# Fixing TensorE's issue order across the turns of an interleaved mixer stage, and moving a row load and a branch hint in the expert stage

## Chip, core, metric

One core of a Trainium2 chip runs the whole program as a single launch. The metric is device time in microseconds (us). TensorE (PE in the rows; PEld is its weight load) does the matmuls, VectorE (DVE) and ScalarE (ACT) the element-wise work, GpSimd (POOL) some element-wise work and some transfers, SyncE (SP) issues most transfers. Each engine takes its own queue in order.

## What is computed

Three blocks follow one another on a sequence of 512 tokens with 1024 features, in float32:

```
for l in range(2):
    p = h @ w_in[l]                                   # 3888 columns
    ya, yb = hgrn2(pa), gla(pb)                       # chunked gated linear attention
    yc = rwkv7(pc)                                    # delta-rule recurrence
    yd = retention(pd)                                # chunked, with rotary
    h = layer_norm(ALPHA * h + concat(ya, yb, yc, yd) @ w_out[l])
    f = swiglu(h) if l == 0 else moe(h)               # 8 experts, top 2 of them
    h = layer_norm(ALPHA * h + f)
h = h + 0.5 * rms_norm(swiglu(rms_norm(h)))           # then a hybrid block:
h = h + rms_norm(concat(rg_lru, window_attention) @ w_o)
h = h + 0.5 * rms_norm(swiglu(rms_norm(h)))
```

Every head of the four mixers of a layer ends in a norm over its 64 features (`rms_norm` or `group_norm`); the keys of rwkv7 are normalized per head as well.

## The kernel before

Activations lie feature-major, as 8 tiles of 128 features by 512 tokens. Weights come as units of 128x1024 over SP's queue (L662, L721 for the experts). Each unit is split into a rounded part on ScalarE and the remainder on VectorE (L353, L354), and a product is three matmuls, high by high, low by high and high by low (L384 to L386; L444 to L447 for the first blocks, L870 to L872 for projections with tokens on the partitions).

**The mixers** (`mixer1`, run for l = 0 and l = 1) are three Python generators that trace instructions: one runs the two rwkv pairs, one the input projections, one the linear attentions (`hg(0)`, `hg(1)`) and retention (`ret`). Each `yield` ends a turn and hands back a cost; `weave` gives the next turn to the stream whose weighted sum of costs is lowest. One turn of the projections is one block of three matmuls. Turns of the other two streams are groups of small products: 32x32 and 64x64 pieces of the chunk solves (L1152, L1092, L1105, L1233), levels of the gated attention (L1343, L1372 to L1411), attention times values (L1423, L1502).

The order in which the weave traces is not the order in which the engines run. A planner places each engine's instructions: it keeps the dependencies and, among what its model takes to be ready, prefers what was traced first. `tc.issue_after(ins)` adds to each instruction that its block traces on the engine of `ins` an edge that puts it behind `ins` in that engine's queue; nobody waits for `ins` to finish by it.

The norm per head is one function, called in one go between two yields (so within one turn), twice in each of the two rwkv pairs (L1058 to L1060 and L1249 to L1250), four times in `hg`, twice in `ret`: 10 calls in each of the two mixers.

```
def head_rstd(self, sq, eps, floor=None):
    s = k.bankB()[:, :P]
    for i in range(NT):
        nc.tensor.matmul(s[32 * i:32 * i + 32], self.bones[:, 48:80], sq[...], ...)      # L924
    nc.scalar.activation(rows, s, AF.Copy)                                               # L926
    nc.tensor.transpose(st, rows, k.ident)                                               # L928
    nc.vector.tensor_scalar(r, st, 1.0 / 64, eps, ...)                                   # L932 (L934 with a floor)
    nc.vector.reciprocal(r, r)                                                           # L935
    nc.scalar.activation(rb, r..., AF.Sqrt)                                              # L936
    for i in range(NT):
        nc.tensor.transpose(R[...], rb[...], k.ident)                                    # L939
```

The output projection of a mixer (`gemm_fm` with `yH`, `yL`) is traced behind the weave and is in no turn.

**The experts** (`experts`): 8 experts one after the other, each with 11 blocks of hidden features (`hidden` for gate and up, L1920 to L1926) and then 11 blocks of the down product (`moe_down`). A block's GpSimd product `rest` (L1935) reads the tiles `mg`, of which there are four; ScalarE's next eviction into `mg` (L1925) needs a free one. Between the blocks `tick` issues side work on GpSimd, in expert 0 the scatter of token rows and gates to DRAM (L1792). `inputs(e + 1)` loads the next expert's rows (L1825, L1827), for expert 1 over GpSimd's own queue, and transposes them on TensorE during the down product (L1836; blocks 4, 6 and 8 in expert 0). In the last block of the last expert every engine loads the largest count of tokens into a register (L1956) and branches around `moe_overflow` (L1957), which runs only where an expert got more than 160 tokens. `combine` follows (L2002 to L2038).

Of the kernel before, what the change touches and what calls it, by code (L numbers as in the profile page):

```python
# [2 lines left out]

# [1 line left out]

# [13 lines left out]
T = 512  # L19
# [7 lines left out]
NE = 8  # L27
# [4 lines left out]
LIM = CAP  # L32
# [700 lines left out]
WEAVEA = (1.0, 1.4, 1.8)  # L733
WEAVEB = (1.0, 1.3, 1.8)
NH32 = 4
WARM = 10
AHEAD = 1
STEP, LAG, LEAD = 4, 12, 4
RINGD, RINGO = 10, 8
LAG1, LEAD1, LAG2 = 12, 2, 18  # L740
LATE = ((0, 2, 4, 6), (0,))
INPUTS, INPUTS0, PLACES = (2, 5, 8), (4, 6, 8), 9
REST, PACE = 4, 8
WARMR = (9, 6)
WARMC = 10
# [45 lines left out]
        return self.pool.tile(shape, dt, name=name, tag=self.tag, bufs=self.bufs)  # L791


def weave(streams, weights):


    at = [0.0] * len(streams)
    live = set(range(len(streams)))
    now = 0.0
    while live:  # L800
        for n in sorted(live, key=lambda i: at[i]):
            try:
                c = next(streams[n])
            except StopIteration:
                live.remove(n)
                break
            if c is not None:
                now = at[n]
                at[n] += c / weights[n]
                break  # L810
            at[n] = max(at[n], now)
# [707 lines left out]
def mixer1(k, l, begin):  # L1519
    tc = k.tc  # L1520
    with tc.tile_pool(name="mxc", bufs=1, reuse_waits="tile") as cp, \
            tc.tile_pool(name="mxa", bufs=1, reuse_waits="tile") as ap, \
            tc.tile_pool(name="mxb", bufs=1, reuse_waits="tile") as bp:
        sl = Slots(ap, "a", NA)
        st = k.stream(f"win{l}")
        if begin:
            k.load_x(sl, st)
        m = Mix(k, l, st, cp, ap, bp)
        if begin:
            trig(k, sl)  # L1530

        def chain(*gens):
            for g in gens:
                yield from g

        weave([chain(m.rwkv_pair(0), m.rwkv_pair(1)),
               chain(m.rwkv_in((6, 2, 0, 4, 5)), m.hg_in(0), m.rwkv_in((7, 8, 3, 1)), m.hg_gate(0), m.hg_in(1),
                     m.hg_gate(1), m.ret_in()),
               chain(m.hg(0), m.hg(1), m.ret())], (WEAVEA, WEAVEB)[l])
        sT = []  # L1540
        for f in range(0, KT, 2):
            t = m.a2(("ZR", "MB")[f // 4], [P, 2, T])
            sT += [t[:, 0], t[:, 1]]
        st = k.ln_stats(sl, 1 if l else 2)
        ws = k.stream(f"wout{l}", *(() if l else (Slots(bp, "b", NB), 0, KT - 2)))
        tot = Totals(*st)
        ys = (lambda q: m.yH[q]), (lambda q: m.yL[q])
        ro = k.moe if l else None
        if ro:
            flat = lambda t: t.rearrange("p a b c -> p (a b c)")  # L1550
            ro.open(sl, *[Cut(flat(m.a2("ZL", [P, NT, 2, P]))) for _ in range(2)])
        for f in range(KT):
            k.resid_in(f, sT)
            if f >= st[0].last and not l:
                continue
            ps = k.gemm_fm(ws, ys, KT, tot.first if f == KT - 1 else None)
            k.resid_out(f, ps, sT, st)
            if ro:
                ro.logits(f, sT[f])
        if ro:  # L1560
            ro.route(sT, tot, ap, m.yH[0])
        else:
            k.ln_end(ws, ys, KT, 2 * KT, sT, k.par(f"ln1g{l}"), k.par(f"ln1b{l}"), sl, st)
        if "y" in k.dbgs:
            for f in range(KT):
                t = sl.tile([P, T])
                k.nc.vector.tensor_tensor(t, m.yH[f].bitcast(F32), m.yL[f].bitcast(F32), op=OP.add)
                k.nc.sync.dma_start(k.dbgs["y"][f], t)
# [26 lines left out]
class Moe:  # L1595
# [251 lines left out]
    def experts(self):  # L1847
# [49 lines left out]
        with tc.tile_pool(name="me", bufs=1, reuse_waits="tile") as me, \  # L1897
                tc.tile_pool(name="mr", bufs=1, reuse_waits="tile") as mr:
            ws = self.ws
            ws.enter(mr)  # L1900
            nxt = self.xe0
            slow = [gains(), residual()]
            for e in range(NE):
                xe = nxt
                beside = [self.scatter(), self.slot_gates(me)] if e == 0 else [clear()] if e == 1 else [collect()] if e == NE - 1 else slow

                def tick(after):
                    with tc.issue_after(after.ins):
                        while beside and next(beside[0], beside) is beside:
                            beside.pop(0)  # L1910

                xf = xe.rearrange("p k w c -> p k (w c)")

                def hidden():
                    ps = k.bankA()[:, :2 * C]
                    for q in range(KT):
                        wH, wL = ws.block()
                        last = q == KT - 1
                        if last:
                            mm(ps[:, :C], wL, xe[:, q, 0], start=False, stop=False, skip_group_check=True)  # L1920
                        mm(ps, wH, xf[:, q], start=q == 0, stop=last, skip_group_check=True)  # L1921
                        if not last:
                            mm(ps[:, :C], wL, xe[:, q, 0], start=False, stop=False, skip_group_check=True)  # L1923
                    a = me.tile([P, C], F32, name="mg", tag="mg", bufs=4)
                    nc.scalar.activation(a, ps[:, C:], AF.Copy)  # L1925
                    V.tensor_tensor(a, ps[:, :C], a, op=OP.add)  # L1926
                    return a

                hid = me.tile([P, NHE, 2, P], F32R, name="hid")
                rest = me.tile([P, NHE, CR], F32, name="rest")  # L1930
                for hb in range(NHE):
                    g = hidden()
                    nc.scalar.activation(g, g, AF.Silu)
                    u = hidden()
                    last = pin(nc.gpsimd.tensor_tensor(rest[:, hb], u[:, P:], g[:, P:], op=OP.mult))  # L1935
                    V.tensor_tensor(u[:, :P], u[:, :P], g[:, :P], op=OP.mult)
                    k.split(u[:, :P], hid[:, hb, 0], hid[:, hb, 1])
                    tick(last)
                    if 0 < e < NE - 1 and hb == NHE - 2:
                        step = self.inputs(e + 1, me)  # L1940
                        next(step)
                if e == 0:
                    step = self.inputs(1, me)
                    next(step)
                if e + 1 < NE:
                    nxt = next(step)

                def side(hb):
                    tick(after[0])
                    if e + 1 < NE and hb in (INPUTS if e else INPUTS0):  # L1950
                        after[0] = next(step)
                    if e + 1 == NE and hb == PLACES:
                        at.append(places())
                    if e + 1 == NE and hb == NHE - 1:
                        with tc.issue_after(ws.last.ins):
                            rv = nc.values_load(self.most[0:1, 0:1], min_val=0, max_val=T)  # L1956
                        with tc.If(rv > LIM):  # L1957
                            moe_overflow(k, h, acc, self.govf, lnrow + [me.tile([P, D], F32, name="yr")])

                at, after = [], [last]  # L1960
                yb, rb = moe_down(k, ws, hid, rest, side)
                gs = [self.gs[:, n, e:e + 1] for n in range(2)]
                if e + 1 < NE:
                    moe_store(k, yb, rb, gs, me, k.yg[e * C:(e + 1) * C])
                else:
                    cp = at[0]
            for n in range(2):
                for w, b in ((0, yb[n]), (1, rb)):
                    if n and w:
                        continue  # L1970
                    hi, lo = cp[:, w, n, 0], cp[:, w, n, 1]
                    nc.scalar.activation(hi, b, AF.Copy, scale=gs[w])
                    V.scalar_tensor_tensor(lo, b, gs[w], hi.bitcast(F32), op0=OP.mult, op1=OP.subtract)
# [83 lines left out]
def moe_down(k, ws, hid, rest, side):  # L2057
# [12 lines left out]
    for hb in range(NHE):  # L2070
# [6 lines left out]
                    r0 = 32 * (2 * n + b % 2)  # L2077
                    mm(rb[r0:r0 + CR], rest[:, b], raws[b][:, n * 512:(n + 1) * 512], start=b < 2, stop=b >= NHE - 2, **kw)
        last = hb == NHE - 1
        side(hb)  # L2080
        (wH, wL), = cut[hb]
        for n in range(2):
            c = slice(n * 512, (n + 1) * 512)
            mm(yb[n], hid[:, hb, 0], wH[:, c], start=hb == 0, stop=False, **kw)
            mm(yb[n], hid[:, hb, 1], wH[:, c], start=False, stop=False, **kw)  # L2085
            mm(yb[n], hid[:, hb, 0], wL[:, c], start=False, stop=last, **kw)
    return yb, rb
# [70 lines left out]
class Second:  # L2158
# [96 lines left out]
    def mixer(self):  # L2255
        k, tc = self.k, self.k.tc
        with tc.tile_pool(name="m2y", bufs=1) as big:
            with tc.tile_pool(name="m2", bufs=1, reuse_waits="tile") as pool:
                m = Hybrid(k, self, big, pool)
                weave([m.project(), m.lru(), m.heads(0), m.heads(1), m.attend()], WEAVE2)  # L2260
            with tc.tile_pool(name="m2o", bufs=1) as p:
                ws = k.stream("wo2", p, RINGO, KT - 2)
                self.post(ws, ((lambda a: m.yH[a]), (lambda a: m.yL[a])), KT, 2, 2 * KT, "mpost", 1.0, "pre2", p, LEAD)
# [289 lines left out]
```

## Time and profile before

| | us |
|---|---|
| runs | 2668.97, 2675.64, 2676.03; median 2675.64 |
| the profiled execution | 2673.79, its span 2672.0 |
| mixers without their first blocks, 28 to 345 and 772 to 1095 | 317 and 323 |
| experts, 1150 to 1720 | 570 |
| TensorE busy | 2599.1 (97%) |
| VectorE, ScalarE, GpSimd busy | 1630.6, 1343.1, 306.6 |

The row of a view gives an engine, the line in the kernel, the operation and the tiles it writes and reads. A wait is put down to the instruction whose end released it; "issue" is time in which an engine waited for nothing that the profile shows, and a q behind an engine's name is its sequencer. PEclk is the mean granted TensorE clock of a stretch: 1.00 is 2.4 GHz, 0.50 is 1.2 GHz.

### The profile page before, as it was taken

To read this page: it belongs to the slowest core of one execution; us is meant where nothing else is said; L and a number is where in the kernel's file an instruction comes from. 1 tells how busy PE (TensorE), PEld (TensorE's weight loads), DVE (VectorE), ACT (ScalarE), POOL (GpSimd) and SP (SyncE) were. 2 spreads that over 40 slices of the span, in tenths; PEclk is the share of its full clock that TensorE was granted. 3 is DMA by queue.
4 is the path that set the end of the run, shared out by engine and by line. 5 is a ranking of instruction groups with operands and counts; after the bars stand their busy time and mean duration, and the time that the engine had idled before them with its cause. 6 is when DMAs were issued, how large, how long until landed. Compare 5 with 4: busy or idle time off the path is not lost. (4 is left out here: it accounts for less than half of the span.)

```text
span 2672.0 us, 48382 instructions
## 1 busy us (share of the span) xinstructions
PE 2599.1 (97%) x18694; PEld 2124.3 (80%) x18694; DVE 1630.6 (61%) x3390; ACT 1343.1 (50%) x2789; POOL 306.6 (11%) x390
## 2 busy tenths in 40 slices
PE   8999999999999999989999999999999999999998
PEld 6776688888877676788888888688888877888887
DVE  6665574444476555557888888665553578655533
ACT  5465354343353554356666776554433467544432
POOL 1101120000031010033233233100000100100000
PEclk9999999999999999999999999899999999999999
DMA  4111422322321112279887888623223212223222
GB/s 160 50 49 50 158 77 97 102 96 95 110 74 43 55 54 69 80 247 288 277 273 268 282 274 266 190 72 102 95 95 100 84 64 77 74 95 101 97 95 71
DMA packets 96330, 334.40 MB, mean 125 GB/s; under 512 B 12079, under 2 KB 15631, under 8 KB 96096
## 3 DMA queue, kind: packets, MB, share of 16 engines
q1 hardware_dynamic: 87520, 305.61, 34.1%
q0 software_dynamic: 8000, 24.95, 3.0%
q8 instruction: 150, 2.46, 0.4%
q10 hardware_dynamic: 576, 0.69, 0.1%
q14 instruction: 84, 0.69, 0.1%
HBM read 313.76 MB, written 17.45 MB: 124 GB/s over the span
## 5 line engine op out<-in xcount | busy, mean ns | idle before, releaser
L353 ACT ACTIVATE whi<-wraw 128x256 fp32r<-128x256 f32 x1172 | 475.6, 415 | 776.7 <-PE bkA L385 706.1
L354 DVE TENSOR_TENSOR wlo<-wraw,whi 128x256 fp32r<-128x256 f32 x1172 | 486.7, 423 | 582.4 <-ACT whi L353 560.1
L384 PE MATMUL bkA<-xH,whi 128*128 128x512 f32 x1352 | 537.4, 397 | 2.1 <-DVE sh L963 1.8
L385 PE MATMUL bkA<-xL,whi 128*128 128x512 f32 x1352 | 535.9, 396 | 0.0
L386 PE MATMUL bkA<-xH,wlo 128*128 128x512 f32 x1352 | 531.9, 393 | 0.0
L1921 PE MATMUL bkA<-xe,mhi 128*128 128x320 f32 x1392 | 361.4, 345 | 10.4 <-ACT mhi L353 8.9
L384 PEld LDWEIGHTS bkA<-xH,whi 128*128 128x128 f32 x1352 | 254.4, 188 | 69.0 <-issue 13.6
L385 PEld LDWEIGHTS bkA<-xL,whi 128*128 128x128 f32 x1352 | 254.8, 188 | 58.4 <-issue 9.6
L386 PEld LDWEIGHTS bkA<-xH,wlo 128*128 128x128 f32 x1352 | 254.4, 188 | 58.4 <-issue 7.0
L1923 PE MATMUL bkA<-xe,mlo 128*128 128x160 f32 x1218 | 289.0, 237 | 2.1 <-DVE mlo L354 2.1
L1921 PEld LDWEIGHTS bkA<-xe,mhi 128*128 128x128 f32 x1392 | 252.0, 190 | 12.2 <-ACT mhi L353 9.5
L1923 PEld LDWEIGHTS bkA<-xe,mlo 128*128 128x128 f32 x1218 | 234.4, 192 | 3.4 <-DVE mlo L354 3.2
L384 PE MATMUL bkA<-hH,whi 128*128 128x512 f32 (+1 forms) x548 | 204.2, 373 | 0.0
L385 PE MATMUL bkA<-hL,whi 128*128 128x512 f32 (+1 forms) x548 | 203.9, 372 | 0.0
L386 PE MATMUL bkA<-hH,wlo 128*128 128x512 f32 (+1 forms) x548 | 203.7, 372 | 0.0
L354 DVE TENSOR_TENSOR mlo<-mraw,mhi 128x1024 fp32r<-128x1024 f32 x105 | 139.9, 1334 | 33.4 <-ACT mhi L353 31.2
L353 ACT ACTIVATE mhi<-mraw 128x1024 fp32r<-128x1024 f32 x105 | 110.3, 1053 | 19.1 <-PE bkA L2085 9.8
L354 DVE TENSOR_TENSOR mlo<-wraw,mhi 128x1024 fp32r<-128x1024 f32 x79 | 104.3, 1323 | 23.7 <-ACT mhi L353 21.8
L385 PEld LDWEIGHTS bkA<-hL,whi 128*128 128x128 f32 x548 | 103.2, 188 | 18.0
L384 PEld LDWEIGHTS bkA<-hH,whi 128*128 128x128 f32 x548 | 103.2, 188 | 18.0
L386 PEld LDWEIGHTS bkA<-hH,wlo 128*128 128x128 f32 x548 | 103.1, 188 | 17.9
L354 DVE TENSOR_TENSOR mlo<-mlow,mhi 128x1024 fp32r<-128x1024 f32 x78 | 105.8, 1358 | 18.3 <-ACT mhi L353 17.0
(738 smaller groups left out, 4428.5 us busy)
## 6 DMA issues: line engine op xcount, KB each, us to landing
mraw<-moew SPq DMA_DIRECT2D x105, 512.0 KB
wraw<-moew SPq DMA_DIRECT2D x81, 512.0 KB
mlow<-moew SPq DMA_DIRECT2D x78, 512.0 KB
wraw<-win SPq DMA_DIRECT2D x76, 512.0 KB
wraw<-f0gu SPq DMA_DIRECT2D x44, 512.0 KB
wraw<-f1gu SPq DMA_DIRECT2D x44, 512.0 KB
wraw<-f2gu SPq DMA_DIRECT2D x44, 512.0 KB
wraw<-f0d SPq DMA_DIRECT2D x22, 512.0 KB
```

The costliest lines, as they stand in the source:

```text
L353: nc.scalar.activation(hi, x, AF.Copy)
L354: nc.vector.tensor_tensor(lo, x, hi.bitcast(F32), op=OP.subtract)
L384: mm(ps, wH, xH, start=first, stop=False)
L385: mm(ps, wH, xL, start=False, stop=False)
L386: mm(ps, wL, xH, start=False, stop=last)
L1921: mm(ps, wH, xf[:, q], start=q == 0, stop=last, skip_group_check=True)
L1923: mm(ps[:, :C], wL, xe[:, q, 0], start=False, stop=False, skip_group_check=True)
```

## The change

`weave` gets the tile context and a distance. It notes the last TensorE instruction of each turn that traced one, and traces each turn under `issue_after` of the note `behind` turns back. Both mixers pass 1, so that all TensorE instructions of a turn stand behind the last of the turn before. The hybrid block passes 10**6, which leaves its order free. In the experts, the row load for expert 1 is put behind the last `rest` of expert 0 on GpSimd; the count is loaded into registers in down block 2 of expert 0, the first matmul of that block being kept in program order; and in down block 6 of the last expert a hint "LikelyTaken" for the branch is put on TensorE behind that block's first matmul.

```diff
+BEHIND = 1
-INPUTS, INPUTS0, PLACES = (2, 5, 8), (4, 6, 8), 9
+INPUTS, INPUTS0, PLACES, HINT = (2, 5, 8), (4, 6, 8), 9, 6
-def weave(streams, weights):
+def weave(tc, streams, weights, behind):
+    traced = tc.nc.cur_bb.bb.instructions
+    ends = []
+
+    def turn(s):
+        n = len(traced)
+        with tc.issue_after(ends[-behind]) if len(ends) >= behind else nullcontext():
+            c = next(s)
+        new = [i for i in traced[n:] if i.engine == mybir.EngineType.PE]
+        if new:
+            ends.append(new[-1])
+        return c
...
-                c = next(streams[n])
+                c = turn(streams[n])
...
-               chain(m.hg(0), m.hg(1), m.ret())], (WEAVEA, WEAVEB)[l])
+               chain(m.hg(0), m.hg(1), m.ret())], (WEAVEA, WEAVEB)[l], BEHIND)
...
                 if e == 0:
                     step = self.inputs(1, me)
-                    next(step)
+                    with tc.issue_after(last.ins):
+                        next(step)
...
                 def side(hb):
                     tick(after[0])
+                    if e == 0 and hb == 2:
+                        counts.append(nc.values_load(self.most[0:1, 0:1], min_val=0, max_val=T))
+                        return pin
+                    if e + 1 == NE and hb == HINT:
+                        return ahead
...
                     if e + 1 == NE and hb == NHE - 1:
-                        with tc.issue_after(ws.last.ins):
-                            rv = nc.values_load(self.most[0:1, 0:1], min_val=0, max_val=T)
-                        with tc.If(rv > LIM):
+                        with tc.If(counts[0] > LIM, label="overflow"):
                             moe_overflow(k, h, acc, self.govf, lnrow + [me.tile([P, D], F32, name="yr")])
+
+                def ahead(m):
+                    with tc.issue_after(m.ins):
+                        tc.mark_branch_hint_location("overflow", "LikelyTaken", [mybir.EngineType.PE])
...
-        side(hb)
+        queued = side(hb)
...
-            mm(yb[n], hid[:, hb, 0], wH[:, c], start=hb == 0, stop=False, **kw)
+            m = mm(yb[n], hid[:, hb, 0], wH[:, c], start=hb == 0, stop=False, **kw)
+            if queued and n == 0:
+                queued(m)
...
-                weave([m.project(), m.lru(), m.heads(0), m.heads(1), m.attend()], WEAVE2)
+                weave(tc, [m.project(), m.lru(), m.heads(0), m.heads(1), m.attend()], WEAVE2, 10 ** 6)
```

## Rows read from the trace of the kernel before

**Rows 1.** The page, busy time of each engine
```profile
PE 2599.1 (97%) x18694; PEld 2124.3 (80%) x18694; DVE 1630.6 (61%) x3390; ACT 1343.1 (50%) x2789; POOL 306.6 (11%) x390
```

**Rows 2.** Stretches: length, busy time by engine, PEclk, DMA; both mixers, hidden of expert 0
```profile
28.00:345.00 317.00, 306.17 (x4001) 224.52 (x4000) 186.51 (x436) 162.59 (x322) 28.63 (x49) 0.98 0.24 78
772.00:1095.00 323.00, 309.59 (x4005) 225.14 (x4005) 187.01 (x443) 160.48 (x316) 21.79 (x35) 0.97 0.19 59
1150.00:1218.00 68.00, 56.69 (x390) 53.04 (x389) 40.13 (x70) 38.63 (x76) 29.84 (x34) 0.90 0.86 240
```

**Rows 3.** TensorE's waits: total us, times, longest us
```profile
PE bkA L1921 <- ACT mhi L353: 8.9, 3, 4.9
...
PE bkB L1152 <- issue: 7.1, 6, 2.2
PE bkB L1372 <- issue: 3.3, 3, 1.9
```

**Rows 4.** Timeline of all engines, one head norm of hg(0): start us, us
```profile
116.32 0.43 PE L924 MATMUL bkB<-hr,ca 128*32 128x128 f32 x8
...
116.67 0.50 PE L384 MATMUL bkA<-xH,whi 128*128 128x512 f32 x1
...
116.87 0.28 ACT L926 ACTIVATE hr<-bkB 128x128 f32<-128x128 f32 x1 [0.26 <-PE bkB L924]
...
117.25 0.28 PE L928 MATMUL bkB<-ca,hr 128*128 128x128 f32 x1
...
118.05 1.28 ACT L936 ACT_TABLE_LOAD   x1 [0.90 <-DVE hr L935]
...
119.35 0.63 ACT L936 ACTIVATE hr<-hr 128x512 f32<-128x512 f32 x1
...
119.90 0.40 PE L385 MATMUL bkA<-xL,whi 128*128 128x512 f32 x1
...
120.13 0.60 PE L939 MATMUL bkB<-ca,hr 128*128 128x128 f32 x4
```

**Rows 5.** TensorE's timeline: first and last step of the shortest and longest head norm
```profile
269.55 0.43 PE L924 MATMUL bkB<-gn,ca 128*32 128x128 f32 x8
...
272.80 0.66 PE L939 MATMUL bkB<-ca,gn 128*128 128x128 f32 x4
...
901.80 0.43 PE L924 MATMUL bkB<-kk,ca 128*32 128x128 f32 x8 [0.35 <-ACT kk L1058]
...
906.83 0.66 PE L939 MATMUL bkB<-ca,kk 128*128 128x128 f32 x4
```

**Rows 6.** Groups of instructions: updates between levels of the gated attention, busy and mean ns
```profile
L1356 DVE TENSOR_TENSOR Qp<-Qp,Dd 128x512 f32<-128x512 f32 x42 | 29.1, 692 | 3.2 <-PE bkB L1400 2.4 <-PE bkB L1392 0.8
...
L1357 DVE TENSOR_TENSOR KX<-KX,Dd 128x256 f32<-128x256 f32 x42 | 19.5, 465 | 0.0
```

**Rows 7.** Stretches, as in rows 2: an idle one with what follows; another idle one
```profile
806.90:809.20 2.30, 0.09 (x11) 0.01 (x2) 0.00 (x0) 0.37 (x1) 0.00 (x0) 0.69 0.00 0
807.80:814.60 6.80, 5.41 (x75) 4.22 (x74) 1.18 (x3) 0.42 (x1) 0.00 (x0) 0.50 0.06 13
1694.00:1696.20 2.20, 0.12 (x4) 0.05 (x3) 1.08 (x3) 0.13 (x1) 0.36 (x1) 1.00 1.02 412
1696.20:1700.00 3.80, 3.80 (x16) 2.48 (x17) 1.65 (x3) 2.18 (x3) 0.00 (x0) 1.00 1.03 422
```

**Rows 8.** GpSimd's timeline in expert 0
```profile
1174.11 1.39 POOL L1792 DMA_INDIRECT xg<-hTok,ii  x1 [0.30 <-issue]
1188.69 0.57 POOL L1825 DMA_DIRECT2D xra<-xg  x1 [13.20 <-DMA xg<-hTok,ii]
...
1189.83 0.26 POOL L1935 TENSOR_TENSOR rest<-mg 128x32 f32<-128x32 f32 x1
...
1216.70 0.36 POOL L1935 TENSOR_TENSOR rest<-mg 128x32 f32<-128x32 f32 x1 [3.19 <-DVE mg L1926]
```

**Rows 9.** Line 1935 in 1150 to 1260: who waited for it (us, times)
```profile
  ACT mg L1925: 21.4, 4
```

**Rows 10.** DMA issues in 1150 to 1260: KB each, median us to landing
```profile
xrb<-xg POOLq DMA_DIRECT2D x4, 32.0 KB, 9.0
```

**Rows 11.** Line 1957: duration ns min/median/max, first and last start
```profile
L1957 PEldq COMPARE_BRANCH  x1: 5426/5426/5426, 1713.9 to 1713.9; - x1
```

**Rows 12.** Timeline behind the branch
```profile
1717.18 1.25 ACT L1972 ACTIVATE last<-bkA,gs 128x512 fp32r<-128x512 f32 x2
...
1719.68 0.76 PE L2002 MATMUL bkB<-last 128*128 128x512 f32 x1 [2.55 <-PEq L1957]
```

More of the change, by code (lines that the diff above doesn't have):

```diff
@@ L1 @@
 import math
-from contextlib import ExitStack
+from contextlib import ExitStack, nullcontext
 import numpy as np
@@ L1534, in chain @@
                 yield from g
-        weave([chain(m.rwkv_pair(0), m.rwkv_pair(1)),
+        weave(tc, [chain(m.rwkv_pair(0), m.rwkv_pair(1)),
                chain(m.rwkv_in((6, 2, 0, 4, 5)), m.hg_in(0), m.rwkv_in((7, 8, 3, 1)), m.hg_gate(0), m.hg_in(1),
                      m.hg_gate(1), m.ret_in()),
-               chain(m.hg(0), m.hg(1), m.ret())], (WEAVEA, WEAVEB)[l])
+               chain(m.hg(0), m.hg(1), m.ret())], (WEAVEA, WEAVEB)[l], BEHIND)
         sT = []
@@ L1901, in experts @@
             nxt = self.xe0
-            slow = [gains(), residual()]
+            slow, counts = [gains(), residual()], []
             for e in range(NE):
```

## Prediction

> **What bounds the kernel now.** I read the busy times first: TensorE is busy 97% of the span, every other engine at most 61% [rows 1]. So the time is TensorE's queue, and an edit can only change its work, its clock or its gaps. This change adds no matmul. The next view is that of stretches [rows 2]: in the mixers TensorE is busy 306 of 317 us and 310 of 323, 24 us idle together, at a granted clock of 0.98 and 0.97; in the hidden part of expert 0 it is busy 57 of 68 us at 0.90. The view of waits [rows 3] says what the idle time is: before the small products of the mixers mostly "issue", 10.4 us in the two rows shown, and before the experts' products ScalarE's splits, 8.9 us. The timeline then shows what keeps the mixers so full [rows 4]. A head norm is a chain through three engines: eight products of L924, ScalarE, one transpose of L928, VectorE, a table load and a square root on ScalarE, four transposes of L939. From the first to the last of its steps it takes 3.8 us here, and TensorE works through it: the projection's matmuls start behind L924 (116.67) and go on to 119.90, 14 of them. They belong to turns traced later. All 20 chains look so, from 3.25 us to 5.03 us from L924 to L939 [rows 5], with 11 to 20 full-width matmuls inside; only in the last one of each mixer are these of the output projection.
>
> **Mixers: the chains.** Behind the change the whole chain is one turn, and all of the next turn's TensorE instructions stand behind its last transpose of L939. TensorE then waits twice within the turn, with every projection block queued behind it: from the end of L924 (116.75) to L928 (117.25), 0.5 us, and from the end of L928 (117.53) to L939 (120.13), 2.6 us [rows 4]: 3.1 us a chain. The table load (1.28 us) and the square root (0.63) are in the second wait and don't get shorter; what ScalarE and VectorE fit in between makes up the rest. The matmuls that lay there are not saved, they run later. The last chain of each mixer keeps its cover, since the output projection is in no turn. So 18 x 3.1 = **+56 us**. The shortest chain would leave 3.25 - 0.43 - 0.28 = 2.5 us idle, the longest 5.03 - 0.71 = 4.3 [rows 5]: 46 to 78 us.
>
> **Mixers: other waits across turns.** Between two levels of the gated attention VectorE needs 0.69 + 0.47 us for the two updates [rows 6], and the weave puts about one or two token-projection turns between, some 0.4 to 0.7 us of matmuls; so far the planner put in as many as were needed. With about 8 levels in each of four parts and 0.4 us short on average this is 13 us. The serial state steps (L1233) and the evictions before a chain add a little, the small wait rows of before fall in with these; I take **+20 us**, between 0 (VectorE ahead everywhere) and 45 (three times the shortfall).
>
> **Mixers: issue waits.** The weave spreads the small products between projection blocks, where before two or three groups of L1152 and L1092 stood together. If the "issue" idle time comes from many short instructions in a row, it shrinks: **-7 us**, between 0 and the 10.4 of [rows 3]. The Trainium skill ("Runtime: NRT & Kernel Launch", Instruction fetch mechanics) says that sequential instruction fetch is hidden by the pace of issue. By it nothing is to be had here and the sum would be 7 us higher. The rows of this case show idle stretches of up to 2.2 us under "issue", without their cause.
>
> **Mixers: the clock.** After an idle stretch of 2.2 us in mixer 1 the granted clock stood at 0.50 for 6.8 us; after another of 2.1 us in the experts it stayed at 1.00 [rows 7]. A chain with 3.1 us of idle time in 4 is more like the first. Half the time at 1.2 GHz is lost where TensorE has work: at most 3.4 us a chain, at least 0. I take 1.5 us, 27 us for 18, and subtract 10 us of the loss that rows 2 have already (0.02 x 317 + 0.03 x 323 = 16 us), as it stands behind the issue waits: **+17 us**, between -16 and +61. The Trainium skill ("TensorE: Matmul & The Clock Gate", HAM oscillation) charges a kernel that pauses in each round with half of its lowered time each time. With 6.8 us for each of 18 chains that is the upper end, a rival below.
>
> **Experts: the row load.** In expert 0 the load L1825 stands in GpSimd's queue at 1175.5 and waits until 1188.69 for the scatters to land; `rest` waits behind it to 1189.83 [rows 8], the four `mg` tiles run out, ScalarE waits 21.4 us for `rest` [rows 9], the splits behind that in ScalarE's queue come late, and TensorE stands. Behind the change the load is issued after the last `rest`, when the scatters have landed. That could give back the idle time of that stretch, 68 - 56.7 = 11.3 us, and half of its low clock, 0.10 x 68 = 6.8: 18 us. But the eight gate scatters of 1 to 2 us each still hold `rest` back, and the rows must arrive before block 4 of the down product, 8.5 us behind the last `rest` (1216.7), while such a load took 9.0 us to land [rows 10]. I take **-8 us**, between -18 and +4 (the whole stretch; transposes that wait for rows).
>
> **Experts: count and hint.** The register load moves to expert 0 and stands on each engine's sequencer, where the engines' queues cover it: 0. TensorE's branch takes 5.4 us from 1713.9 [rows 11] and leaves a gap of 2.55 us [rows 12]. With the target fetched early, L2002 would still wait for ScalarE's first eviction, 1717.18 + 0.63: some 0.1 us later it could start, 1.7 us sooner than 1719.68. I take **-2 us**, between 0 and -10 (if the half-clock stretch of the following combine went too).
>
> **Sum.** 56 + 20 - 7 + 17 - 8 - 2 = +76 us on the profiled execution's 2673.8 us: **2750 us**. That execution is 1.8 us below the median of the runs, which is inside their spread.
>
> **Rivals.**
> *The clock falls after every chain* for 6.8 us and all of it costs: 18 x 3.4 = 61 instead of 17, 2794 us, more with long chains. For it: the stretch in mixer 1; against it: the one in the experts, and low time that falls into another wait. 0.2.
> *The waits are mostly covered*: chains at 2.5 us, no level waits, the clock as now: 46 - 7 - 8 - 2 = +29, 2703 us. 0.14.
> *Faster.* The chains cost little and the supply of short instructions was what mattered: then 10.4 us of issue waits go, with them the 16 us of low clock, and the expert edits give 10: -36 us, 2637 us. It decides where a chain leaves less than 36 / 18 = 2.0 us idle; the table load and the square root alone are 1.9 [rows 4], so nearly all else would have to vanish, or the edges would have to let later blocks into a turn. 0.10.
> *The order hardly changes*, since the planner did much the same before: only the experts' -10, 2664 us. Against it: 14 blocks inside a chain are from later turns [rows 4]. 0.04.
>
> **How the numbers follow.** The forecast itself, 2715 to 2780 us, has 0.5; 0.02 is left for worse than all this. The lower end of the range leaves out the last two rivals and half of the covered case's lower side, the upper one most of what lies above long chains with a clock that falls each time: 2690 to 2825. A measurement of this kernel tells some 0.3%, 8 us, from no change. Faster by more than that: 0.10 plus half of the unchanged order, 0.12; within it 0.03; slower 0.85.
>
> **What would show it.** Right: L924, L928 and L939 without projection matmuls between them and with idle rows behind "ACT L926" and "ACT L936" of about 0.5 and 2.6 us in 18 chains; PEclk below 0.97 in both mixers; L1825 behind the last `rest` and no wait for L1935 on ScalarE; a gap under 1 us before L2002. Wrong: projection matmuls inside the chains still, or mixers whose length grew by less than 20 us each although the idle rows are there, which would mean that work came in elsewhere.

## The result and the profile after

| | before | after |
|---|---|---|
| median of the runs, us | 2675.84 (2668.97 to 2676.71) | 2838.97 (2835.9 to 2849.35) |
| profiled execution, us | 2673.8, span 2672.0 | 2836.8, span 2835.0 |

After to before is 1.063 (95% interval 1.061 to 1.065): 163 us slower, where 74 were forecast. The sign was right, the size wrong; 2839 lies above the range.

The page of the changed kernel, its busy times and the granted clock in 40 slices:

```profile
PE 2683.3 (95%) x18694; PEld 2179.1 (77%) x18694; DVE 1639.9 (58%) x3390; ACT 1349.3 (48%) x2789; POOL 305.7 (11%) x390
...
PEclk9986799999998986999999999999999999999999
```

The instruction counts are those of [rows 1], yet TensorE is busy 84 us longer. PEclk has its low digits in the two mixers, slices 2 to 4 and 12 to 15 (counted from 0), a 6 in each.

The view of stretches, cut at the same three places in both kernels: from the start to the first product of mixer 1's first kk norm, on to the first hidden product of expert 0, on to the end. Columns are start and end, length, busy time and instructions of the five engines, PEclk, DMA share and GB/s. Before:

```profile
0.00:779.90 779.90, 757.72 (x6215) 605.40 (x6215) 422.12 (x1029) 360.99 (x783) 73.38 (x122) 0.99 0.28 94
779.90:1157.10 377.20, 364.61 (x4336) 274.95 (x4337) 210.43 (x524) 181.16 (x355) 21.61 (x34) 0.97 0.20 63
1157.10:2660.80 1503.70, 1476.82 (x8148) 1243.93 (x8146) 993.58 (x1832) 800.97 (x1653) 209.68 (x233) 0.99 0.47 156
```

After:

```profile
0.00:868.80 868.80, 800.73 (x6193) 633.92 (x6193) 425.41 (x1028) 362.97 (x781) 72.39 (x122) 0.92 0.25 85
868.80:1336.30 467.50, 415.66 (x4355) 307.77 (x4356) 217.36 (x525) 184.61 (x357) 19.50 (x34) 0.86 0.14 46
1336.30:2823.80 1487.50, 1466.95 (x8147) 1237.39 (x8146) 992.63 (x1831) 801.73 (x1653) 211.87 (x233) 1.00 0.48 160
```

The first two stretches, with the mixers in them, grew from 1157.1 to 1336.3 us: +179.2. TensorE's busy time there rose from 1122.3 to 1216.4, its idle time (length less busy) from 34.8 to 119.9. So **85 us are waits and 94 us are the same matmuls at a lower clock**: in the two traces' clock records TensorE has 1.2 GHz for 37.5 us of these stretches before and for 259.4 us after. That the new mix of matmuls is dearer by itself is all but ruled out by the same traces: counted with the busy time that each line's matmuls add where the clock is at 2.4 GHz, the two stretches come to 1108 us of work before and 1112 after (an estimate). The third stretch, the experts and all behind them, is 16 us shorter.

What TensorE waited for in 28 to 1336 us of the changed kernel (us in total, times, longest us):

```profile
PE bkB L952 <- ACT hr L949: 20.0, 8, 2.5
PE bkB L937 <- ACT kk L1071: 17.9, 4, 4.5
PE bkB L952 <- ACT kk L949: 13.6, 4, 3.6
PE bkB L1385 <- DVE Qp L1360: 13.3, 5, 6.0
PE bkB L952 <- ACT gn L949: 7.4, 4, 2.5
...
PE bkB L941 <- ACT hr L939: 3.8, 8, 0.6
PE bkB L1385 <- DVE KX L1370: 2.1, 4, 0.6
PE bkB L941 <- ACT kk L939: 1.8, 4, 0.5
...
PE bkB L941 <- ACT gn L939: 1.8, 4, 0.5
PE bkB L1385 <- issue: 1.6, 1, 1.6
...
PE bkB L1165 <- issue: 0.9, 1, 0.9
```

Lines of the mixers are 13 higher than before: L937, L941 and L952 are the three TensorE steps of a head norm (L924, L928, L939 of [rows 4]). The two "issue" rows are those of [rows 3], 10.4 us then and 2.5 now. Sixteen norms wait in their second and third step, 41.0 + 7.4 us. Two more rows were 1.0 us each in the view of before: L937 for ScalarE's Square (17.9 now) and L1385 for VectorE's Qp (13.3 now).

```profile
PE bkB L924 <- ACT kk L1058: 1.0, 3, 0.4
PE bkB L1372 <- DVE Qp L1347: 1.0, 2, 0.7
```

One norm of rwkv in the timeline (start us, us, engine, line; in brackets the idle time before it and what ended it); it answers to [rows 4]:

```profile
152.12 0.43 PE L937 MATMUL bkB<-gn,ca 128*32 128x128 f32 x8
...
153.00 0.33 PE L941 MATMUL bkB<-ca,gn 128*128 128x128 f32 x1 [0.46 <-ACT gn L939]
...
153.85 1.28 ACT L949 ACT_TABLE_LOAD   x1 [0.90 <-DVE hr L948]
155.14 0.63 ACT L949 ACTIVATE gn<-hr 128x512 f32<-128x512 f32 x1
...
155.82 1.12 PE L952 MATMUL bkB<-ca,gn 128*128 128x128 f32 x4 [2.50 <-ACT gn L949]
```

No projection matmul stands in it any more: 0.46 and 2.50 us idle, and the four transposes take 1.12 us where [rows 4] has 0.60. The stretches around it show why:

```profile
153.30:155.80 2.50, 0.03 (x1) 0.00 (x0) 0.37 (x2) 1.91 (x2) 0.00 (x0) 0.79 0.00 0
155.80:161.60 5.80, 5.78 (x16) 4.72 (x17) 2.94 (x5) 2.97 (x6) 0.00 (x0) 0.50 0.00 0
```

The clock falls within the wait and stays at 1.2 GHz for the 5.8 us of work behind it.

### The profile page after: what moved, and what is told of

The parts are those of the page before. It is cut to its first block, busy times and chain, and to the rows that moved or that the text cites. A ratio compares the mean times of both kernels' runs of the same rounds, so it can differ in the third digit from the quotient of the medians.

```text
span 2835.0 us, 48410 instructions
## 1 busy us (share of the span) xinstructions
PE 2683.3 (95%) x18694; PEld 2179.1 (77%) x18694; DVE 1639.9 (58%) x3390; ACT 1349.3 (48%) x2789; POOL 305.7 (11%) x390
## 5 line engine op out<-in xcount | busy, mean ns | idle before, releaser
L384 PE MATMUL bkA<-xH,whi 128*128 128x512 f32 x1352 | 560.2, 414 | 2.1 <-DVE sh L976 1.8
L386 PE MATMUL bkA<-xH,wlo 128*128 128x512 f32 x1352 | 539.3, 399 | 0.0
L384 PEld LDWEIGHTS bkA<-xH,whi 128*128 128x128 f32 x1352 | 261.2, 193 | 78.4 <-issue 21.5
L386 PEld LDWEIGHTS bkA<-xH,wlo 128*128 128x128 f32 x1352 | 261.4, 193 | 58.0 <-issue 1.9
L385 PEld LDWEIGHTS bkA<-xL,whi 128*128 128x128 f32 x1352 | 261.8, 194 | 52.9 <-issue 4.0
L354 DVE TENSOR_TENSOR mlo<-mraw,mhi 128x1024 fp32r<-128x1024 f32 x105 | 139.8, 1333 | 39.3 <-ACT mhi L353 37.0
L354 DVE TENSOR_TENSOR mlo<-mlow,mhi 128x1024 fp32r<-128x1024 f32 x78 | 105.7, 1357 | 18.7 <-ACT mhi L353 16.5
```

What stands on the lines that cost most here:

```text
L354: nc.vector.tensor_tensor(lo, x, hi.bitcast(F32), op=OP.subtract)
L384: mm(ps, wH, xH, start=first, stop=False)
L385: mm(ps, wH, xL, start=False, stop=False)
L386: mm(ps, wL, xH, start=False, stop=last)
```

## The experiments

Theory at the start: all of the loss is the strict order of the mixers' turns; a wait that a turn keeps to itself costs its length, and then the clock behind it. The rivals: waits alone; the experts' edits; and, for the clock, not the waits but the mix of matmuls that the strict order makes. In the tables, "idle" and "busy" are TensorE's in the first two stretches, worked out for each run as above.

### Which edit it is

The free weave with the experts' edits, by one constant:

```
-BEHIND = 1
+BEHIND = 10 ** 6
```

> The changed kernel with the mixers' turns free again (BEHIND so large that no turn waits for another); the experts' row load and branch hint stay as changed. Theory (all of the loss is the strict order, the experts' edits give back about 9 us: the hidden matmuls of expert 0 after its row load took 59 us in place of 68): 2660 to 2670 us, and both mixers look as they did before the change (TensorE idle 11 and 13 us, clock 0.98). Rival (the experts' edits bring nothing or cost something): 2675 us or more.

Measured 2658.6 us, 0.9956 of before (0.9943 to 0.9970). Its first two stretches are 1158.0 us, 1118.7 busy and 39.3 idle, those of before within the spread; the third is 1494.3. The order carries all of the loss, and without it the kernel is faster than the one before, too.

The strict order with the experts as before (their three edits undone in the changed kernel):

```
-    with tc.issue_after(last.ins):
-        next(step)
+    next(step)
...
-        counts.append(nc.values_load(...))      # early count, and the branch hint below it
...
+        with tc.issue_after(ws.last.ins):
+            rv = nc.values_load(...)
```

> The kernel before with the strict order of the mixers' turns alone: row load, count and branch of the experts as before. Theory (order +172, experts' edits -9): 2844 to 2852 us, with the 8.9-us wait of the hidden matmuls for ScalarE's mhi and the 2.6-us gap ahead of the scaling of the last rows back. Rival (the experts' edits are worth nothing): 2839 us.

Measured 2843.6 us, 1.0664 of before (1.0637 to 1.0691) against 1.0628 for the whole change (1.0606 to 1.0650). By the medians the experts' edits are worth 10 us under the strict order too; the two intervals overlap. The first two stretches:

```profile
0.00:867.70 867.70, 798.63 (x6193) 631.76 (x6193) 425.67 (x1028) 363.57 (x781) 72.37 (x122) 0.93 0.26 85
867.70:1323.70 456.00, 400.41 (x4355) 295.86 (x4356) 217.19 (x525) 184.17 (x357) 20.00 (x34) 0.89 0.16 52
```

The mixers are those of the changed kernel, yet TensorE is busy 1199.0 us in them, not 1216.4: one order, and the clock's part is 77 us over before in this execution and 94 in the other. So a difference of less than some 17 us in busy time between two single executions tells nothing.

The row load alone, then the count with the hint alone, in the free weave:

```
 if e == 0:
     step = self.inputs(1, me)
-    next(step)
+    with tc.issue_after(last.ins):              # first run
+        next(step)
...
+    counts.append(nc.values_load(...))          # second run: early count
...
+    tc.mark_branch_hint_location("overflow", "LikelyTaken", [mybir.EngineType.PE])
```

> The kernel before with one edit of the experts alone: expert 1's row load issued behind expert 0's last product on GpSimd. Weave, count and branch as before. Theory (the 8.9-us wait of the hidden matmuls for ScalarE's mhi goes, and the clock that fell behind it): -7 to -10 us of the 2673, ratio 0.9965 (0.996 to 0.9975). Rival (the gain of the free weave with both edits is in the count and the hint): 1.000.

> The kernel before with the other two edits of the experts alone: the count read early in expert 0 and the branch hint for TensorE queued in the last expert. Theory (the gap of 2.6 us ahead of the scaling of the last rows shrinks to about 1.5 us, nothing else): -1 to -3 us, ratio 0.9992 (0.9985 to 1.0). Rival (it carries most of the 11.7 us): 0.9965 or less.

Measured 2665.9 us, 0.9964 (0.9949 to 0.9980), and 2674.9 us, 1.0005 (0.9990 to 1.0019). The row load carries the gain. The hidden part of expert 0 and its down product as two stretches, before:

```profile
1152.30:1215.80 63.50, 52.19 (x357) 50.02 (x355) 38.34 (x67) 35.34 (x69) 28.68 (x31) 0.89 0.90 255
1215.80:1238.40 22.60, 22.60 (x123) 14.64 (x123) 15.63 (x18) 12.33 (x16) 9.29 (x9) 1.00 0.86 314
```

With the row load alone:

```profile
1154.40:1201.40 47.00, 46.35 (x354) 45.54 (x352) 36.43 (x64) 33.96 (x67) 28.73 (x26) 1.00 0.98 306
1201.40:1230.70 29.30, 25.50 (x124) 15.92 (x124) 17.57 (x21) 14.64 (x21) 11.73 (x14) 0.94 0.91 306
```

The hidden part gives back its idle time, 10.7 us, and 5.8 us of busy time at the clock it has now; the down product pays 6.7 us for it, since the transposes of expert 1's rows wait for the later load, and the clock falls with it:

```profile
PE bkB L1849 <- DMA xra<-xg: 3.6, 1, 3.6
```

Count and hint: nothing that these runs can tell from zero.

### What a head norm costs under a fence

The free weave, with only the norms fenced: a norm's sums issue behind all turns traced before, and all turns traced behind a norm issue behind its last transpose.

```
 def turn(s):
-    with tc.issue_after(ends[-behind]) if len(ends) >= behind else nullcontext():
+    with tc.issue_after(NORM[-1]) if NORM else nullcontext():     # last transpose of the last norm
         c = next(s)
...
 # head_rstd: the sums stand behind the end of every turn since the last norm
+with ExitStack() as es:
+    for q in list(ENDS):
+        es.enter_context(k.tc.issue_after(q))
     for i in range(NT):
         nc.tensor.matmul(s[32 * i:32 * i + 32], self.bones[:, 48:80], ...)
```

> The free weave (with the experts' edits) in which only the head norms are fenced: each norm's sums issue behind every turn traced before them, and every turn traced behind a norm issues behind its last transpose. In TensorE's order 16 of the 20 chains have nothing in their waits, as under the strict order; all other turns are free. It prices the first term of the prediction by itself. Theory (chains cost the waits, 48 us by the rows of the changed kernel, and the clock behind them, 25 us by the run that filled them): 2659 + 73 = 2732 us (2715 to 2750). Rival (the waits cost their length and no clock): 2707 us. Rival (a chain's wait is regained later because the other turns catch up): 2675 us or less.

Measured 2759.3 us, 1.032 of before (1.030 to 1.034), above the expected range: 100 us more than the free weave in which it was made. Its first two stretches:

```profile
0.00:824.20 824.20, 765.23 (x6197) 608.57 (x6197) 426.80 (x1028) 362.60 (x781) 73.42 (x122) 0.97 0.27 89
824.20:1260.10 435.90, 394.15 (x4355) 292.29 (x4356) 214.92 (x525) 183.95 (x357) 20.66 (x34) 0.91 0.16 49
```

Against the free weave that is 61 us more idle (100.7 less 39.3) and 41 us more busy. Sixteen fenced norms alone thus make 102 us, where the strict order makes 179. The waits ahead of a norm belong to its price; the theory had left them out:

```profile
PE bkB L947 <- ACT kk L1083: 17.8, 4, 4.5
```

The same norms in the changed kernel, with their waits filled by matmuls whose output nobody reads, so that the chain stays as long as it is but TensorE works:

```
         nc.tensor.matmul(s[32 * i:32 * i + 32], ...)
+    hot = k.warms(3, q.ins)             # 3 of 128x512 into a spare bank, behind the sums
...
     nc.tensor.transpose(st, rows, k.ident)
+    hot = k.warms(11, q.ins)            # 11 more, ahead of the last four transposes
```

> The changed kernel with 3 matmuls of 128x512 into a spare bank behind the sums of each head norm and 11 behind its first transpose (14 x 0.213 = 3.0 us at full clock), pinned there, so that TensorE works through the waits of all 20 chains. They compute nothing that is used. Chains stay as long as they are. Theory (the chains' waits bring the clock down): outside the two stretches of 54.6 us the mixers spend some 148 us at the lower clock, 114 more than before the change; at 0.47 us each up to 54 us less if chains cause all of it, 27 if half: 2785 to 2815 us. Rival (a wait costs its own length and no clock): 2839 to 2850 us, the dummies being about 0.5 us longer than the idle time of a chain.

Measured 2814.7 us, 1.054 of before. The first two stretches:

```profile
0.00:861.30 861.30, 816.49 (x6337) 646.75 (x6337) 426.98 (x1028) 362.37 (x781) 72.25 (x122) 0.95 0.25 85
861.30:1312.90 451.60, 419.52 (x4495) 312.03 (x4496) 216.99 (x525) 184.44 (x357) 18.70 (x34) 0.94 0.15 47
```

The 280 added matmuls by themselves, in the same stretches (TensorE's columns and the clock):

```profile
0.00:861.30 861.30, 39.37 (x140) 27.11 (x140) 0.95 0.25 85
861.30:1312.90 451.60, 39.24 (x140) 26.99 (x140) 0.94 0.15 47
```

They are busy 78.6 us, of which 9.1 lie over other matmuls. Without them TensorE is busy 1166.7 us, 50 us less than in the changed kernel, with the same work in the same order (32 less than in the run of the order alone). The kernel gets 24 us faster by doing some 70 us more. That waits cost no clock is refuted: the clock around the norms costs 41 us by the run before, which has the waits ahead of the norms in it, and 32 to 50 by this one.

### Where else TensorE waits

A norm in three turns, so that others' turns stand in its waits, the order still strict:

```
     nc.scalar.activation(rows, s, AF.Copy)
+    yield 0.8
...
     nc.scalar.activation(rb..., r..., AF.Sqrt)
+    yield 1.2
     R = k.bankB()
```

> The changed kernel, strict order kept, but a head norm is three turns and not one (a yield of 0.8 behind its first copy and one of 1.2 behind its Sqrt, none of 2.0 at the end), so that turns of other streams stand between its TensorE steps: 3 projection matmuls in each wait of most hg chains, 6 in the gn chains, 6 to 9 in two of the four kk chains. Theory (the strict order costs the waits that a turn keeps to itself, and the clock that falls behind them): 10 hg chains x 1.3 us + 4 gn chains x 2.6 + kk 7 = 30 us of the 48 us of chain waits covered, and of the 25 us that filling all chains gave back in clock some 15: 2794 us (2775 to 2812). Rival (only waits, no clock): 2809 us. Rival (the loss is the thin mix of products that the strict order makes): no more than 10 us gained.

Measured 2791.7 us, 1.045 (1.042 to 1.048), as expected.

The Square that opens a kk norm, moved to the head of its turn on ScalarE:

```
 def rwkv_pair(self, p):
     r, kr = self.x[p], self.x[2 + p]
+    kk = self.a("kk")
+    act(kk, kr, AF.Square, scale=kkp)
     y, ya = k.bankB(), k.bankB()
```

> The changed kernel, strict order kept, with the Square that opens each kk norm moved to the head of rwkv_pair, so that on ScalarE it stands ahead of the two Tanh and of the Exp that waits for VectorE's scan, and no longer behind them. Theory (TensorE's 17.9 us at the first matmuls of the four kk norms are ScalarE's queue): those four waits fall to under 1 us each and some of the clock's 10.2-us falls there shorten, -14 to -18 us of waiting and -5 to -12 of clock: 2812 us (2805 to 2822). Rival (the wait is for the projection that feeds the Square): no change, 2839 us.

Measured 2823.2 us, 1.056 (1.054 to 1.059), 1 us above the expected range. The row of 17.9 us is gone; ScalarE's queue was what the four first products waited for. Part came back in the same norms, further on (1.8 and 13.6 us in the changed kernel):

```profile
PE bkB L952 <- ACT kk L949: 16.0, 4, 4.0
...
PE bkB L941 <- ACT kk L939: 4.8, 4, 1.5
```

In the profiled execution, the fastest of four at 2811.2 us, all idle time together fell by only 5 us and the busy time by 21. How much of the median's 16 us is clock is not shown.

The distance of the fence, 2 and 4 turns in place of 1:

```
-BEHIND = 1
+BEHIND = 2                                      # then 4
```

> The changed kernel with BEHIND = 2. In TensorE's order 2 projection matmuls stand in the first wait of some ten chains, 0 to 3 in the second, none in the kk chains. Theory (uncovered waits and the clock behind them): between one and four turns of slack, 2790 us (2765 to 2815). Rival (any fixed order loses the same): 2825 us or more.

> The changed kernel with BEHIND = 4: a turn is issued behind the turn four places ahead of it in the traced order. In TensorE's order 2 projection matmuls now stand in the first wait of 14 of the chains and 1 to 10 in the second, the four kk chains have none. Theory (waits that a turn keeps to itself, and the clock behind them): most chain waits and the waits for Qp and X half covered, the kk ones not: idle time of the mixers from 108 to about 50 us, the lower clock's time about halved, 2740 us (2700 to 2780). Rival (any fixed order loses its 160 us, since the runs of projection matmuls are cut): 2810 us or more.

| runs | median, us | to before | idle, us | busy, us |
|---|---|---|---|---|
| changed kernel, 1 turn | 2839.0 | 1.063 | 119.9 | 1216.4 |
| order alone, 1 turn | 2843.6 | 1.066 | 124.7 | 1199.0 |
| 2 turns | 2787.7 | 1.043 | 106.4 | 1177.6 |
| 4 turns | 2757.6 | 1.032 | 86.8 | 1173.1 |
| free | 2658.6 | 0.996 | 39.3 | 1118.7 |

The loss shrinks with the slack, in both columns (in the busy time not clearly from two turns to four), and even four turns keep about 100 us of it: the kk norms, with nothing in their waits still, hold L952 12.8 us and L937 11.5 us.

### The two stretches of 54.6 us

In the changed kernel the clock stays down for 54.6 us in either mixer, from 243.5 and from 1086.6 us, which lie within the 5.4- and 6.0-us waits of hg(1) for Qp. The table of clocks in mixer 1, changed kernel:

```profile
1094.00:1104.00 10.00, 8.93 (x222) 7.33 (x218) 4.20 (x12) 0.20 (x1) 0.00 (x0) 0.50 0.01 3
...
1114.00:1124.00 10.00, 9.91 (x96) 7.96 (x97) 1.77 (x4) 3.00 (x6) 0.96 (x2) 0.50 0.09 26
```

The run of the order alone traces the mixers alike, waits 6.01 us at the same place, and the same products start at 1088.9 us there:

```profile
1114.00:1124.00 10.00, 9.69 (x140) 6.90 (x138) 2.79 (x6) 4.96 (x11) 1.07 (x3) 1.00 0.11 32
```

One order, one kind of work, two clocks: up again after 20.5 us here, after 54.6 there (in mixer 0 it was down for 54.6 us in both). From these products to the long wait of the next norm it takes 46.3 us in this run and 60.2 in the changed kernel, so 34 us more at 1.2 GHz cost 14. The waits at the start, filled with 25 matmuls, then also the next gap, with 9 more:

```
 # hg(1), ahead of the first scores (25) and, in the second run, of the first level too (9)
+hot = k.warms(25) if part else None
```

> The changed kernel with 25 matmuls of 128x512 into a spare bank (25 x 0.213 = 5.3 us at full clock) issued ahead of the first score matmul of hg(1), so that TensorE isn't idle while it waits 5.4 and 6.0 us for VectorE's Qp there. They compute nothing that is used. Theory (the two stretches of 54.6 us at 1.2 GHz that begin behind these waits are started by the waits): both stretches run at 2.4 GHz or nearly; over the mixers TensorE's busy time rose 105 us for some 223 us more at the lower clock, 0.47 us for each, so 2 x 54.6 x 0.47 = 51 us less, 2788 us (2775 to 2805). Rival (the mix of 256-column and small products lowers the clock by itself): the stretches stay at 0.5, 2836 to 2845 us.

> The changed kernel with 25 matmuls of 128x512 ahead of hg(1)'s first scores, as in the run before, and 9 more (1.9 us) ahead of its first level, where the run before still had gaps of 1.41 and 1.68 us and the clock fell at 242.98 and 1082.66 us, behind them. Nothing that they compute is used. Theory (a wait of TensorE starts the fall, and the mix of 256-column and small products keeps whatever clock it finds: the same order ran at 1.2 GHz for 54.6 us in one run and for 20.5 us in another): neither mixer has the stretch of over 50 us; 46.3 us in place of 60.2 us from the first level's products to the next chain, so 2 x 12 to 2 x 20 us less than 2823, 2780 to 2800 us. Rival (the mix brings the clock down without a wait): both stretches of about 50 us are still there, 2820 to 2830 us.

Measured 2822.7 and 2830.2 us. In the first run both stretches were still there, 51.2 us each, behind gaps of 1.41 and 1.68 us. In the second one was left, of 44.4 us from 255.3, with no gap over 0.90 us in the 10 us ahead of it; in mixer 1 the clock was down for 10.2 us only. Neither theory is borne out as it stood: the first time lies between the two, and the second is that of the rival with one of its two stretches gone.

Three more runs: hg(1) one long empty turn later, so that real work fills the wait; 32 matmuls amid the stretch; and token projections in turns of 12 matmuls instead of 3.

```
 yield from self.wait(lambda: part in self.hgi)                   # hg, first run
+if part:
+    yield 5.0
...
+hot = k.warms(32) if part and n == 2 and not u else None         # third level, second run
...
-yield 0.5 * GEMM_US                                              # proj_tok, third run
+if kk % 4 == 3:
+    yield 2.0 * GEMM_US
```

> The changed kernel, strict order kept, with hg(1) starting one empty turn of weight 5.0 later, so that 33 token-projection matmuls and two or three small products stand ahead of its first scores, which waited 5.4 and 6.0 us for VectorE's Qp. Theory A (the wait starts the long stretches): the wait falls to under 1 us in both mixers and neither has a stretch over 30 us: -11 us of waiting and -25 to -45 of clock, 2775 to 2805 us. Theory B (the mix of three token matmuls and one group of small products, turn by turn, takes the clock down also without a long wait): the waits go and stretches of 40 us or more are still there, 2820 to 2830 us.

> The changed kernel with 32 matmuls of 128x512 into a spare bank amid the long stretch at 1.2 GHz, ahead of the third level of hg(1), some 12 us behind its start; nothing that they compute is used. Theory (once it is down the clock stays down in the thin mix of token projections and small products, and once it is up it stays up): the clock comes back during the 32 matmuls and stays, so each stretch of 54.6 us becomes one of 20 to 30 us; 2 x 28 us x 0.48 = 27 us less, 2 x 9 us more for the added matmuls: 2830 us (2820 to 2840). Rival (the mix itself takes the clock down again): within some 10 us of the added matmuls it falls again and the stretches add up to 45 us or more in each mixer, 2850 to 2860 us.

> The changed kernel, strict order kept, with the token projections in turns of 12 matmuls of 256 columns (a yield of 2.0 products behind every fourth) in place of 3; the same matmuls, the same waits ahead of hg(1), longer runs between the small products, as the free weave has them. Theory (short runs of projection matmuls between the small products keep the clock down behind a fall): the clock falls behind the 5.4- and 6.0-us waits and is back within 20 us in both mixers, 2 x 34 us x 0.48 = 33 us less, 2806 us (2795 to 2820). Rival (the length of the runs is nothing to it): stretches of about 50 us, 2835 to 2845 us.

Measured 2816.7, 2850.2 and 2836.0 us. With hg(1) late, whose two runs (2807.8 and 2825.6 us) lie 18 us apart and so decide nothing by their time, the waits were 2.4 and 2.1 us, not under 1, and stretches of 51.2 and 41.0 us came with them: the long wait is not needed. With the 32 matmuls, mixer 0:

```profile
250.00:260.00 10.00, 10.00 (x72) 8.36 (x72) 1.47 (x4) 0.60 (x1) 0.00 (x0) 0.81 0.00 1
260.00:270.00 10.00, 7.63 (x283) 6.05 (x281) 5.82 (x16) 0.00 (x0) 1.79 (x4) 1.00 0.01 3
270.00:280.00 10.00, 9.55 (x64) 7.92 (x64) 1.28 (x4) 3.28 (x7) 5.73 (x13) 0.54 0.21 55
```

The clock comes up within them, after 10.2 us in place of 54.6 (13.7 in mixer 1); 17 us later, behind waits of 0.5 to 1.1 us, it is down again for 34.1 us, in mixer 1 for 23.9. The theory that the mix keeps the clock that it finds falls with this: here it came down in the mix with short waits alone. With long token turns no stretch is over 17.1 us, and TensorE is busy 38 us less than in the changed kernel; but its idle time rises by 28 us to 148, since hg's small products now wait for VectorE between levels (up to 1.8 us), and the time is the same. The Trainium skill ("TensorE: Matmul & The Clock Gate", A second HAM failure mode: psum-queue depth-cycling) tells of a kernel whose clock goes to and fro because TensorE idles briefly between groups of matmuls, without a long wait. The falls behind 0.5 to 1.1 us here agree. What exactly brings the clock back in one run and not in another, with the same order, stays open.

## Why the prediction was wrong in size

**The failed step is the clock**: "I take 1.5 us, 27 us for 18 ... +17 us, between -16 and +61". It measured 94 us, and 77 in the run of the order alone, above its upper end both times. The part at the norms was under-sized: 32 to 50 us for 16 norms, 2.0 to 3.1 us each, while the row chosen for it [rows 7] was the right one. The rest, about half of the 94 us, was not in the sum at all: the step counted falls behind the norms only. The strict order puts three or six projection matmuls between small products where the planner had often put a dozen and more, and leaves short waits between them; there the clock falls too, and comes back late. (In mixer 0, 83 of 120 runs of projection matmuls are of three or six and 14 of twelve or more; before, 29 and 28 of 98.) What each of these causes has of the rest is not shown. The two stretches of 54.6 us are the worst of it, some 22 us each at the price of the pair above (an estimate: 54.6 x 14 / 34).

**The chains: right.** 18 x 3.1 = 56 us were forecast, 16 x 3.0 = 48 measured (41.0 + 7.4). In each mixer not one but two last norms kept their cover. The trace of before has a hint of it, since the last but one of mixer 0 (from 317.94 us) already holds 8 matmuls of the output projection. Its longest norm is that from 985.61 us, 5.16 us and not the 5.03 of [rows 5], which moves the upper end by 2 us only. The table load and the root are in the second wait, 2.50 us, as said.

**Other waits: the term was too small**, +20 with an upper end of 45; by the idle time it is 85 - 48 + 8 = 45. And it named the wrong ones. The updates between levels, 13 us in the sum, wait 2.1 us at L1385 for KX. What came was a turn's first product waiting for another engine's queue: the Square behind two Tanh, a scan and an Exp (17.9 us), and Qp behind the gate's activations (13.3 us). Before, the planner had put projection blocks there, and [rows 3] has nothing of it. The sentence that waves these through is "the small wait rows of before fall in with these".

**Issue waits: right**, -7 forecast, -7.9 in the two rows of [rows 3]; what they are made of stays open.

**The row load: right**, -8 forecast, 0.9964 of before measured, which is -10 us; both of its parts showed, 16.5 us given back (18 at most by the prediction) and 6.7 paid for rows that come late. On ScalarE the wait for `rest`, 21.4 us in [rows 9], became this (us, times):

```profile
  ACT mg L1938: 7.5, 3
```

**Count and hint:** -2 forecast, no difference measured. TensorE's branch went from 5.4 us [rows 11] to 0.5, and the gap ahead of the first combine product [rows 12] shrank from 2.55 to 1.32 us, not to under 1:

```profile
L1974 PEldq COMPARE_BRANCH  x1: 502/502/502, 1886.2 to 1886.2; - x1
...
1891.34 0.50 PE L2024 MATMUL bkB<-last 128*128 128x512 f32 x1 [1.32 <-ACTq L1974]
```

TensorE now waits there for ScalarE's own branch, and one product later 0.7 us for VectorE's (L1974 as well), so that of the 2.5 us only 0.5 are gone: the prediction had left these two branches out.

So 48 + 45 - 8 + 94 = 179 in the mixers and -16 behind them, 163. Of the 16, the run of the row load alone shows 10; the rest is not told from the spread. Of the **rivals**, that of the clock falling after every chain was the nearest (2794 us): it held the mechanism, but tied it to the chains. "Mostly covered", "faster" and "the order hardly changes" fell with the first timeline. The range failed because its upper end was built from the clock's price per norm alone, and lay below the sum of the terms' own upper ends (78 + 45 + 61 + 4 = 188, 2862 us).

## What to carry to other kernels

A fixed issue order costs on the engine it fixes every wait that the planner used to cover, and that includes the waits of a turn's first instruction for another engine's queue, which the trace before does not list because they were covered. Where TensorE's clock can fall, price an edit that opens many short waits by the busy time as well as by the idle time: here the busy time grew by 94 us (77 in the other run of the order) and the idle time by 85. If an order must be fixed, leave slack (two turns in place of one took 51 us off here) or cut the turns at their waits (47 us off); longer runs of large matmuls between the small products kept the clock up but gained no time, as the waits grew.

## What was not expected of the hardware

TensorE's clock stayed at 1.2 GHz for 54.6 us although, once the wait ahead was over, TensorE was busy 8.9 to 10.0 of every 10 us; work of small products and 256-column matmuls did not bring it back. And the gate's Exp, Ln, Exp on ScalarE needs three table loads in a row. Two of them fall into the 5.4-us wait (241.34 to 246.75) and are 2.56 us of it:

```profile
239.40 1.28 ACT L1322 ACT_TABLE_LOAD   x1
...
241.51 1.28 ACT L1323 ACT_TABLE_LOAD   x1
...
243.45 1.28 ACT L1325 ACT_TABLE_LOAD   x1
...
246.75 0.65 PE L1385 MATMUL bkB<-Qp,KX 64*32 64x32 f32 x32 [5.41 <-DVE Qp L1360]
```

The Trainium skill ("ScalarE: Activation LUTs", Table sets: the hidden batching unit) names a set that holds both functions, so that Ln and Exp share one load; in this build they do not.
